# Building the block-diagonal operands of a state recurrence in four groups of chunks, with the sums on VectorE and the placement on ScalarE

## The chip, the cores and the metric

The kernel is one launch on one core of a Trainium2 chip. The metric is the device time of the launch in microseconds, the median of several runs. Beside the times there is one profiled execution with its trace: for every instruction the engine, its start and duration, and what released it. The engines are TensorE (PE, with its weight loads as PEld), VectorE (DVE), ScalarE (ACT), GpSimd (POOL) and SyncE (SP), which issues nearly all DMAs.

## The reference, cut to what matters

Two blocks of a network on 256 tokens of 1024 features, float32. The first block has a mixer with two branches, a gate and an output product, and a feed-forward layer. The second block has two layers, each with two gated feed-forward parts around a mixer with two attentions. The change lies in the first block's mixer, in its state-space branch:

```
u = rmsnorm(x); proj = u @ w_in; u_ssm, q, k, v = split(proj)       # 512 columns each
a = exp(lam * dt); b = ((a - 1) / lam) * (B_re + i B_im)            # 32 groups, 64 states, 16 channels
x_t = a * x_(t-1) + b u_t;  y_t = Re(C x_t) + D u_t                 # per group, over 256 tokens
y = gelu(y); y = y * sigmoid(y @ w_glu + b_glu)
```

The other branch is a stick-breaking attention over q, k, v (8 heads). The gates are `sigmoid(u @ w_gate + b_gate)`, eight weight blocks.

## The kernel before, in words

**Weights.** All products are float32 in three passes: each weight block of 1 MB is loaded by SP, ScalarE writes its high part (L538), VectorE its low part (L553), both in halves of 1024 columns, and TensorE multiplies high by high, high by low, low by high (L590 to L592). One feature-major block is 48 matmuls of 256 columns. In the first mixer up to three split blocks are held at a time.

**The order.** The tile framework is told to keep the order of emission, so each engine's queue is the order in which the program emits. In the first mixer the class `Flow` writes that order: each stream of work is a generator that yields an engine, a declared time and the buffers it needs (`acc`, `t2`, `t4`), or the name of a signal to wait for. `Flow` keeps a clock for each engine in these declared times, emits the piece that could start first (among pieces close together the one with the lowest priority number), and puts steps of the fillers, which are the large products, where TensorE would otherwise wait. One filler step is two tiles, six matmuls, counted as 2 x 0.327 us. The fillers come in this order: u0, u1 (the recurrence's inputs), qk0 to qk3, the values v, then a barrier "kz", then the eight gate blocks, a barrier "sg", and the rest. `f.free["POOL"] = 5.5` tells `Flow` that GpSimd is busy for 5.5 us with a fill that was emitted just before.

**The recurrence.** It runs over 64 steps of four tokens. `s5_load_bc` issues the DMAs of B and C in SP's queue, behind x, constants and the first three weight blocks. `s5_powers` makes the powers of a: `pw` and `dk`, [128, 4, 2, 16] each (power, real or imaginary, chunk). `s5_c` masks C into `cpad` on GpSimd (L1033, four products), transposes it on TensorE (L1041) and copies it back on ScalarE (L1043). Two operands are block-diagonal, [128, 2, 16, 4, 2, 16], 4096 columns: `s5bb` (B times dk) and `s5wT` (C times pw). Both are filled with zeros by GpSimd, s5bb at the start of the mixer (L1368), s5wT inside `s5_c` (L1049). `s5_part` then makes one of the four powers for all 16 chunks: two products of 512 columns on VectorE (L995), and four sums of 256 columns on 64 partitions on GpSimd, written straight into the diagonal blocks (L998, L999). There are four parts for B and four for C.

When all four parts of B are done, `s5_b` transposes s5bb (L1017, ScalarE copies at L1020) into `bT`, with a signal for each quarter, and `s5_k` multiplies s5bb by C's transpose (L1102, signal "kz"). `s5_states` (four groups of chunks) multiplies the inputs by bT (L1161), turns and scans them on VectorE and GpSimd, and adds their outputs with `s5wT` (L1205, L1208), once all four parts of C are there (signal "wT"). `s5_turns` makes the rotations `csT` (VectorE L1075 to L1078, ScalarE L1081 to L1083). `stick` is one head of the attention: two `t2` buffers from its first product until its last, which needs the values; heads run one at a time. The copies of the inputs u into the steps' layout are 16 ScalarE instructions of 32 partitions for each of u0 and u1 (L1141).

Of the kernel before, what the change touches and what calls it, by code (L numbers as in the profile page):

```python
# [25 lines left out]
# The tail of a layer: its last TAIL row blocks, row by row; the products after which the first row's two  # L26
# halves are transposed, in feed-forward layers and in the others.
# [3 lines left out]
# Of Flow: buffers, priorities, and what it weighs (times in us).  # L31
# [10 lines left out]
# The first block's later products: gates, glu and the two projections.  # L42
LATE = "g0 g1 g2 g3 g4 g5 g6 g7 lu a0 a1 s0 s1".split()
# The weight stream: blocks loaded in halves, tiles split ahead, split blocks at a mixer's end.
# [3 lines left out]
# When a feed-forward layer's first hidden columns are turned (without and with gate), and when the  # L48
# weights of a mixer's first products are taken.
# [4 lines left out]
def host_constants():  # L54
    """Tables that depend on the shapes alone."""
# [39 lines left out]
class Halves:  # L95
    """Columns of a row in two tiles."""
# [10 lines left out]
class Row:  # L107
    """The end of a layer for 128 tokens: their sums on top of the residual, the norm
    (of the root mean square, or of mean and variance when there is a bias) and the
    feature-major split of the result."""  # L110
# [31 lines left out]
    def finish(self):  # L142
        """Up to the scale of the rows; then self.piece(c0, c1) writes the result."""
# [26 lines left out]
    def turn(self, c0, c1, pool=None):  # L170
        """Transposes columns c0:c1 and splits the high parts; returns the low parts' step."""
        k, nc, b = self.k, self.k.nc, self.b
        n = (c1 - c0) // P
        t = slice(b * P, (b + 1) * P)
        ps = (pool or k.mm)("tp")
        for c in range(n):
            nc.tensor.transpose(ps[:, c * P:(c + 1) * P], self.out[:, b, c0 + c * P:c0 + (c + 1) * P], k.ident)  # L177
        q = slice(c0 // P, c1 // P)
        v = ps[:, :n * P].rearrange("p (c t) -> p c t", c=n)
        hi, lo = self.xs[0][:, q, t], self.xs[1][:, q, t]  # L180
        nc.scalar.activation(hi, v, AF.Copy)  # L181
        return lambda: nc.vector.tensor_tensor(lo, v, hi.bitcast(F32), OP.subtract)

    def early(self):
        """All of it but the transposes."""
# [8 lines left out]
    def late(self, head):  # L194
        """All of it, the next layer's work on the other tokens filling the wait."""
# [15 lines left out]
class FFHead:  # L211
    """The first 256 hidden columns of a feed-forward layer, token by token."""
# [40 lines left out]
class MixHead:  # L253
    """The first columns of a mixer's input product, token by token."""
# [21 lines left out]
def act(n, exp=False):  # L276
    """A ScalarE instruction's time, in us, for n columns."""
# [3 lines left out]
def dve(n, fast=False):  # L281
    """A VectorE instruction's time, in us, for n columns."""
# [3 lines left out]
class Flow:  # L286
    """An order of emission for streams of work that share the engines. A stream is a generator that
    yields (engine, time, resources...) before it emits that work, or the name of a signal to wait for;
    the next piece is the one that could start first by a model of the engines, and fillers (feature-major
    products) go where TensorE would wait. Each resource is a count of buffers with the times at which  # L290
    they come free."""
# [24 lines left out]
    def rest(self):  # L316
        """Puts off the current stream, whose products are too small to keep TensorE's clock up."""
# [6 lines left out]
    def start(self, s):  # L324
        """When a stream's next piece could start, or None."""
# [26 lines left out]
    def weight(self, e):  # L352
        """The next part of the weights' split, as a stream's piece."""
# [26 lines left out]
    def filler(self, t):  # L380
        """A step of the first filler."""
# [13 lines left out]
    def evac(self, engine, d, f):  # L395
        """Work that follows the filler's products."""
        self.evacs.append((self.free["PE"] + 0.65, engine, d, f))

    def open(self):
        """Whether a filler can go on."""  # L400
# [51 lines left out]
class Kern:  # L452
    def __init__(self, ctx, tc, A, out):
# [8 lines left out]
        self.blocks = []      # planned weight blocks, in the order of their use  # L462
        self.staged = []      # loaded, not yet split
        self.loaded = 0
        self.pieces = 0       # halves of blocks split so far
# [36 lines left out]
    def rowblk(self, w, r0, nk, c0, n):  # L502
        """nk chunks of 128 rows from r0, n columns from c0, as [128, nk, n]."""
# [26 lines left out]
    def high(self):  # L530
        """The high part of half a weight block."""
# [9 lines left out]
    def piece(self):  # L541
        """The low part of half a weight block, and the high part of the next."""
# [43 lines left out]
    def mm3(self, out, l, r, start, stop, **kw):  # L586
        """out (+)= l.T @ r, the operands split in high and low parts."""
# [6 lines left out]
    def split_from(self, hi, lo, src, scale=None):  # L594
        """hi, lo (float32r) from src (* scale)."""
# [8 lines left out]
    def fm_gen(self, key, xs, evac, alloc=None):  # L604
        """A feature-major block: [128, 256] sums per 128 columns, in PSUM tiles of
        two; evac(i, tile) follows each tile. Yields the tiles of work done."""
# [27 lines left out]
    def fill(self, tiles):  # L634
        """Emits about that much of the waiting work."""
# [9 lines left out]
    def tok_mm(self, o, w, xs, k0, b, c0, c1, first, last, **kw):  # L645
        """Adds a row block to the token-major sums o of the 128 tokens b, columns c0:c1."""
# [9 lines left out]
    def tok_first(self, o, ws, b, n):  # L656
        """The token-major sums o of n columns, the tokens' low parts last."""
# [15 lines left out]
    def tok_tail(self, accs, parts, rows, head, at):  # L673
        """The last row blocks (w, xs, k0): the first 128 tokens, then the others,
        each followed by the end of its row."""
# [24 lines left out]
    def bcast_row(self, src, n, name):  # L700
        """A row of DRAM on every partition."""
# [13 lines left out]
    def transpose_split(self, src, nchunk, xs):  # L715
        """src: [128 tok, 2, nchunk*128] -> split feature-major xs."""
# [155 lines left out]
    # The states' recurrence runs over 64 steps of four tokens each: state' = a^4 state + V [u], and  # L872
    # the outputs of a step are W state + K [u], with V, W and K made of B, C and the powers of a.
    # Its inputs and outputs sit on the partitions as (token of the step, channel of 32).
# [26 lines left out]
    def s5_powers(self, f):  # L901
        """The powers of a and what goes with them: s5c (parameters by state), pw, dk, tau4, r4."""
# [60 lines left out]
        cf = dk[:, 0]  # L963
# [9 lines left out]
        def cmul(out, x, y, n):  # L973
            """out = x * y, complex; x: n numbers per state chunk, y: one."""
# [9 lines left out]
        cmul(dk[:, 1:4], pw[:, 0:3], cf, 3)  # L984
# [3 lines left out]
    def s5_part(self, f, dst, x, y, k, s0, s1):  # L988
        """dst (block-diagonal) = y_k * x; s0, s1: the signs' operations."""
        nc = self.nc  # L990
        TT, GT = nc.vector.tensor_tensor, nc.gpsimd.tensor_tensor
        yield "DVE", 2 * dve(512), "t4"
        t = self.t4([P, 2, 2, 16, 16], "s5p")
        for i in range(2):
            TT(t[:, i], x, y[:, k, i, None, :, None].to_broadcast([P, 2, 16, 16]), OP.mult)  # L995
        yield "POOL", 2.8
# [1255 lines left out]
```

## Time and profile before

| | |
|---|---|
| median of 3 runs | 1560.99 us (1559.63 to 1564.06) |
| profiled execution, first to last instruction | 1560.2 us (no other time of it is listed) |
| mean granted TensorE clock | 0.994 |
| busy: TensorE, VectorE, ScalarE, GpSimd | 1534.7, 992.3, 773.2, 97.8 us |

The median stands 0.8 us above the span of the profiled execution. "Busy" of TensorE counts overlapping matmuls as one stretch, so a busy TensorE need not be at its peak; where the granted clock is low, the same matmuls take longer and count as busy all the while.

### The profile page before, as it was taken

To read this page: it belongs to the slowest core of one execution; us is meant where nothing else is said; L and a number is where in the kernel's file an instruction comes from. 1 tells how busy PE (TensorE), PEld (TensorE's weight loads), DVE (VectorE), ACT (ScalarE), POOL (GpSimd) and SP (SyncE) were. 2 spreads that over 40 slices of the span, in tenths; PEclk is the share of its full clock that TensorE was granted. 3 is DMA by queue.
4 is the path that set the end of the run, shared out by engine and by line. 5 is a ranking of instruction groups with operands and counts; after the bars stand their busy time and mean duration, and the time that the engine had idled before them with its cause. 6 is when DMAs were issued, how large, how long until landed. Compare 5 with 4: busy or idle time off the path is not lost.

```text
span 1560.2 us, 25562 instructions
## 1 busy us (share of the span) xinstructions
PE 1534.7 (98%) x10637; PEld 1418.5 (91%) x10637; DVE 992.3 (64%) x1572; ACT 773.2 (50%) x1259; POOL 97.8 (6%) x112
## 2 busy tenths in 40 slices
PE   8799999999999999999999999999999999999998
PEld 7699989989999998989999999999999999899997
DVE  7956776454654547778875445844557779864544
ACT  7455845444543435557654343534434567554342
POOL 2841000000000000000000000000000000000000
PEclk9899999999999999999999999999999999999999
DMA  7413355556564555532565655565546433565550
GB/s 215 154 62 122 136 197 186 197 172 207 179 225 163 186 183 176 192 103 88 188 216 189 204 175 189 191 210 170 185 152 216 136 108 125 181 225 189 188 190 28
DMA packets 188597, 265.24 MB, mean 170 GB/s; under 512 B 10441, under 2 KB 154817, under 8 KB 188482
## 3 DMA queue, kind: packets, MB, share of 16 engines
q1 hardware_dynamic: 186466, 256.27, 49.7%
q0 software_dynamic: 2016, 7.34, 1.4%
q8 instruction: 84, 1.38, 0.4%
q14 instruction: 31, 0.25, 0.0%
HBM read 262.55 MB, written 1.05 MB: 169 GB/s over the span
## 4 chain that ended last, share of the span: by engine, by line
PE 92%; DVE 4%; POOL 2%; ACT 1%; issue 1%; DMA 0%; DVEq 0%; SPq 0%; ACTq 0%
PE mm L590 16%; PE mm L591 16%; PE mm L592 16%; PE acc L591 8%; PE acc L592 8%; PE acc L590 8%; PE head L664 6%; DVE wsplit L553 1%; PE tp L177 1%; PE cps L1665 1%; PE in L590 1%; PE in L592 1%; PE in L591 1%; PE apt L1949 1%; PE mo L1887 1%
## 5 line engine op out<-in xcount | busy, mean ns | idle before, releaser
L553 DVE TENSOR_TENSOR wsplit<-st,wsplit 128x1024 fp32r<-128x1024 f32 (+1 forms) x482 | 562.0, 1210 | 184.4 <-ACT wsplit L538 184.0
L590 PE MATMUL mm<-xh,wsplit 128*128 128x256 f32 x2000 | 572.2, 286 | 0.0
L591 PE MATMUL mm<-xl,wsplit 128*128 128x256 f32 x2000 | 564.8, 282 | 0.0
L592 PE MATMUL mm<-xh,wsplit 128*128 128x256 f32 x2000 | 564.8, 282 | 0.0
L538 ACT ACTIVATE wsplit<-st 128x1024 fp32r<-128x1024 f32 (+1 forms) x482 | 471.7, 1036 | 30.6 <-DMA st<-in_ffn_wg_dram 11.9
L590 PEld LDWEIGHTS mm<-xh,wsplit 128*128 128x128 f32 x2000 | 378.9, 189 | 4.5 <-issue 1.1
L591 PEld LDWEIGHTS mm<-xl,wsplit 128*128 128x128 f32 x2000 | 379.0, 189 | 2.1
L592 PEld LDWEIGHTS mm<-xh,wsplit 128*128 128x128 f32 x2000 | 378.6, 189 | 0.2 <-DVE wsplit L553 0.2
L590 PE MATMUL acc<-wsplit,ffh 128*128 128x512 f32 x480 | 189.5, 395 | 0.0
L592 PE MATMUL acc<-wsplit,ffl 128*128 128x512 f32 x480 | 189.4, 395 | 0.0
L591 PE MATMUL acc<-wsplit,ffh 128*128 128x512 f32 x480 | 189.3, 394 | 0.0
L828 ACT ACTIVATE fff<-mm 128x512 f32<-128x512 f32 x55 | 32.9, 598 | 280.1 <-PE mm L592 280.1
L832 DVE TENSOR_TENSOR fff<-fff,mm 128x512 f32<-128x512 f32 x55 | 37.9, 688 | 174.4 <-PE mm L592 111.2
L598 ACT ACTIVATE ffh<-fff 128x512 fp32r<-128x512 f32 x55 | 34.8, 632 | 165.8 <-DVE fff L832 165.8
L592 PEld LDWEIGHTS acc<-wsplit,ffl 128*128 128x128 f32 x480 | 90.4, 188 | 21.0
L590 PEld LDWEIGHTS acc<-wsplit,ffh 128*128 128x128 f32 x480 | 90.4, 188 | 18.8
L591 PEld LDWEIGHTS acc<-wsplit,ffh 128*128 128x128 f32 x480 | 90.4, 188 | 18.7
L707 POOL TENSOR_TENSOR rowst<-rowst,neghalf 128x1 f32<-128x1 f32 x18 | 14.7, 817 | 1227.2 <-DVE rowst L154 946.8
L664 PE MATMUL head<-wsplit,xh 128*128 128x256 f32 (+2 forms) x416 | 66.1, 311 | 0.0
L664 PEld LDWEIGHTS head<-wsplit,xh 128*128 128x128 f32 x416 | 59.6, 188 | 3.5
L599 DVE TENSOR_TENSOR ffl<-fff,ffh 128x512 fp32r<-128x512 f32 x55 | 38.1, 693 | 38.4 <-ACT ffh L598 38.4
L181 ACT ACTIVATE xh<-tp 128x256 fp32r<-128x256 f32 (+1 forms) x46 | 18.6, 470 | 48.6 <-PE tp L177 48.6
(405 smaller groups left out, 1894.6 us busy)
## 6 DMA issues: line engine op xcount, KB each, us to landing
st<-in_ffn_wg_dram SPq DMA_DIRECT2D x44, 1024.0 KB, 5.6
st<-in_ffn_wu_dram SPq DMA_DIRECT2D x44, 1024.0 KB, 5.4
st<-in_ffn_wd_dram SPq DMA_DIRECT2D x44, 1024.0 KB, 5.0
st<-in_w_ff_dram SPq DMA_DIRECT2D x32, 1024.0 KB, 6.4
st<-in_w_in_dram SPq DMA_DIRECT2D x23, 1024.0 KB, 6.3
st<-in_w_out_dram SPq DMA_DIRECT2D x12, 1024.0 KB, 4.9
st<-in_w_gate_dram SPq DMA_DIRECT2D x8, 1024.0 KB, 5.5
st<-in_w_in_dram SPq DMA_DIRECT2D x10, 512.0 KB, 5.4
```

The source lines that it names most:

```text
L177: nc.tensor.transpose(ps[:, c * P:(c + 1) * P], self.out[:, b, c0 + c * P:c0 + (c + 1) * P], k.ident)
L181: nc.scalar.activation(hi, v, AF.Copy)
L538: self.nc.scalar.activation(self.split[i][0][:, a, b], self.staged[i][:, a, b], AF.Copy)
L553: self.nc.vector.tensor_tensor(lo[:, a, b], st[:, a, b], hi[:, a, b].bitcast(F32), OP.subtract)
L590: nc.tensor.matmul(out, lh, rh, start=start, stop=False, **kw)
L591: nc.tensor.matmul(out, lh, rl, start=False, stop=False, **kw)
L592: nc.tensor.matmul(out, ll, rh, start=False, stop=stop, **kw)
L598: nc.scalar.activation(hi, src, AF.Copy)
L599: nc.vector.tensor_tensor(lo, src, hi.bitcast(F32), OP.subtract)
L664: self.nc.tensor.matmul(o, l, r, start=i == 0, stop=i == len(ops) - 1)
L828: nc.scalar.activation(f, ps, AF.Silu if gated else AF.Relu)
L832: nc.vector.tensor_tensor(f, f, ps, OP.mult)
```

## The change

`s5_part` makes a group of four chunks for all four powers, instead of one power for all 16 chunks. VectorE does four products of 256 columns and both sums (256 columns each on 128 partitions) into a new `t2` buffer; ScalarE copies the sums into the diagonal blocks, in two instructions of 64 partitions and 512 columns. GpSimd does no sums. To allow this, `dk` is stored in reverse order of the powers, and its three products are made one by one. `s5_b` transposes each group as soon as it is placed and signals its quarter of `bT`; "bb" comes after the last transposes. "wT" is signalled by group, and `s5_states` waits for its own group alone. The zero fills of both operands move to the very start of the program, ahead of the first DMA issue: s5bb and a quarter of s5wT on GpSimd, three quarters of s5wT on VectorE. The line `f.free["POOL"] = 5.5` goes, and so does GpSimd's declared 3.4 us for s5wT's fill.

```diff
@@ s5_powers
-        cf = dk[:, 0]
+        cf = dk[:, 3]
...
-        cmul(dk[:, 1:4], pw[:, 0:3], cf, 3)
+        for k in range(3):
+            cmul(dk[:, 2 - k:3 - k], pw[:, k:k + 1], cf, 1)
@@ s5_part
-    def s5_part(self, f, dst, x, y, k, s0, s1):
+    def s5_part(self, f, dst, x, y, g, s0, s1):
-        TT, GT = nc.vector.tensor_tensor, nc.gpsimd.tensor_tensor
-        yield "DVE", 2 * dve(512), "t4"
-        t = self.t4([P, 2, 2, 16, 16], "s5p")
+        TT = nc.vector.tensor_tensor
+        js = slice(4 * g, 4 * g + 4)
+        yield "DVE", 4 * dve(256) + 2 * dve(256), "t4", "t2"
+        t = self.t4([P, 2, 2, 4, 4, 16], "s5p")
+        u = self.t2([P, 2, 4, 4, 16], "s5u")
         for i in range(2):
-            TT(t[:, i], x, y[:, k, i, None, :, None].to_broadcast([P, 2, 16, 16]), OP.mult)
-        yield "POOL", 2.8
+            for r in range(2):
+                TT(t[:, i, r], x[:, r, js, None, :].to_broadcast([P, 4, 4, 16]),
+                   y(i)[:, :, js].rearrange("p k j -> p j k")[..., None].to_broadcast([P, 4, 4, 16]), OP.mult)
+        TT(u[:, 0], t[:, 0, 0], t[:, 1, 1], s0)
+        TT(u[:, 1], t[:, 0, 1], t[:, 1, 0], s1)
+        f.put("t4")
+        yield "ACT", 2 * act(512)
         for a, h in enumerate((slice(0, 64), slice(64, P))):
-            GT(dst[h, 0, :, :, a], t[h, 0, 0], t[h, 1, 1], s0)
-            GT(dst[h, 1, :, :, a], t[h, 0, 1], t[h, 1, 0], s1)
-        f.cur["ready"] = max(f.cur["ready"], f.free["POOL"])
-        f.put("t4")
+            nc.scalar.activation(dst[h, :, js, :, a], u[h], AF.Copy)
+        f.put("t2")
@@ s5_b
-        for k in range(4):
-            yield from self.s5_part(f, self.bb[:, :, :, 3 - k].rearrange("p i j a c -> p i j c a"), self.s5bn,
-                                    self.dk, k, OP.subtract, OP.add)
+        for g in range(4):
+            yield from self.s5_part(f, self.bb, self.s5bn, lambda i: self.dk[:, :, i], g, OP.subtract, OP.add)
+            if g == 0:
+                self.bT = self.t16([P, 16, 2, P], "s5bT")
+            for j in (4 * g, 4 * g + 2):
+                yield "PE", 0.43, "acc"
...
+                yield "ACT", act(512)
+                nc.scalar.activation(self.bT[:, j:j + 2].rearrange("p j i s -> p (j i s)"), ps, AF.Copy)
+                f.put("acc")
+            f.sig("bT%d" % g)
         f.sig("bb")
...
@@ s5_c
-        yield "POOL", 3.4
-        self.wT = wT = self.t16([P, 2, 16, 4, 2, 16], "s5wT")
-        nc.gpsimd.memset(wT, 0.0)
...
-        for k in range(4):
-            yield from self.s5_part(f, wT[:, :, :, k].rearrange("p i j a c -> p i j c a"), cc, self.pw, k,
-                                    OP.add, OP.subtract)
+        for g in range(4):
+            yield from self.s5_part(f, self.wT, cc, lambda i: self.pw[:, :, i], g, OP.add, OP.subtract)
+            f.sig("wT%d" % g)
         f.put("t2")
-        f.sig("wT")
@@ s5_states
-        yield "wT"
+        yield "wT%d" % g
@@ first_block
         self.consts()
+        self.bb = self.t16([P, 2, 16, 4, 2, 16], "s5bb")
+        nc.gpsimd.memset(self.bb, 0.0)
+        self.wT = self.t16([P, 2, 16, 4, 2, 16], "s5wT")
+        nc.vector.memset(self.wT[:, 0], 0.0)
+        nc.vector.memset(self.wT[:, 1, :8], 0.0)
+        nc.gpsimd.memset(self.wT[:, 1, 8:], 0.0)
...
-        self.bb = self.t16([P, 2, 16, 4, 2, 16], "s5bb")
-        nc.gpsimd.memset(self.bb, 0.0)
-        f.free["POOL"] = 5.5
```

## Rows read from the trace of the kernel before

**Rows 1.** Windows of 10 us: busy by engine (instructions), granted clock, DMA share, GB/s.

```profile
core 0: us, PE busy (x) PEld busy (x) DVE busy (x) ACT busy (x) POOL busy (x), PEclk, DMA share, GB/s
...
30.00:40.00 10.00, 10.00 (x86) 10.00 (x86) 9.64 (x31) 9.77 (x24) 0.37 (x1) 1.00 0.43 132
...
50.00:60.00 10.00, 8.37 (x40) 7.75 (x40) 10.00 (x12) 6.26 (x9) 9.73 (x9) 0.66 0.42 124
60.00:70.00 10.00, 6.72 (x30) 5.27 (x30) 9.83 (x12) 0.78 (x2) 9.73 (x9) 1.00 0.27 91
70.00:80.00 10.00, 7.28 (x32) 6.26 (x33) 9.79 (x7) 3.08 (x4) 9.75 (x8) 0.66 0.67 206
```

**Rows 2.** Waits of TensorE, 40 to 100 us: total, times, longest.

```profile
PE s5ps L1017 <- POOL s5bb L998: 2.7, 1, 2.7
PE sc L1288 <- DVE sa L1284: 2.4, 1, 2.4
PE sz L1268 <- ACT H L1391: 2.4, 1, 2.4
PE s5ps L1017 <- POOL s5bb L999: 1.2, 1, 1.2
```

**Rows 3.** Groups of TensorE's instructions by line, 40 to 100 us.

```profile
L590 PE MATMUL mm<-xh,wsplit 128*128 128x256 f32 x45 | 14.1, 313 | 0.0
...
L590 PE MATMUL mm<-wsplit,xh 128*128 128x512 f32 x16 | 7.3, 454 | 0.0
```

**Rows 4.** The chain that ended last, in order of time: start, us, what.

```profile
94.46 0.81 PE s5k L1102 x8
```

**Rows 5.** Timeline of VectorE: start, us, instruction.

```profile
9.12 3.59 DVE L1352 COPY s5par<-s5par 16x128 f32<-16x128 f32 x1
...
24.74 4.00 DVE L950 TENSOR_SCALAR s5q<-s5q 128x16 f32<-128x16 f32 x1
...
38.20 1.28 DVE L995 TENSOR_TENSOR s5p<-s5bc,s5q 128x512 f32<-128x512 f32 x2
...
47.70 1.22 DVE L553 TENSOR_TENSOR wsplit<-st,wsplit 128x1024 fp32r<-128x1024 f32 x1
...
52.78 2.37 DVE L995 TENSOR_TENSOR s5p<-s5bc,s5q 128x512 f32<-128x512 f32 x2
...
66.46 0.42 DVE L1294 SCALAR_TENSOR_TENSOR szs<-const,szs 128x256 f32<-128x256 f32 x1
66.80 1.77 DVE L553 TENSOR_TENSOR wsplit<-st,wsplit 128x1024 fp32r<-128x1024 f32 x1
```

**Rows 6.** Timeline of GpSimd.

```profile
9.13 3.51 POOL L1368 MEMSET s5bb<- 128x4096 f32 x1
22.00 3.25 POOL L1033 TENSOR_TENSOR s5cpad<-s5bc,const 128x256 f32<-128x256 f32 x4 [9.36 <-DMA s5bc<-in_C_re_dram]
25.19 3.51 POOL L1049 MEMSET s5wT<- 128x4096 f32 x1
...
47.86 1.64 POOL L998 TENSOR_TENSOR s5bb<-s5p 64x256 f32<-64x256 f32 x1 [4.16 <-DVE s5p L995]
...
71.38 1.70 POOL L999 TENSOR_TENSOR s5bb<-s5p 64x256 f32<-64x256 f32 x1
...
81.82 0.74 POOL L999 TENSOR_TENSOR s5wT<-s5p 64x256 f32<-64x256 f32 x1
```

**Rows 7.** Timeline of TensorE.

```profile
15.34 0.58 PE L590 MATMUL mm<-xh,wsplit 128*128 128x256 f32 x1
...
19.13 0.41 PE L592 MATMUL mm<-xh,wsplit 128*128 128x256 f32 x1
...
25.50 0.60 PE L1041 MATMUL s5ps<-const,s5cpad 128*128 128x128 f32 x4
```

**Rows 8.** Timeline of ScalarE.

```profile
20.11 1.28 ACT L940 ACT_TABLE_LOAD   x1
...
23.56 4.48 ACT L1141 ACTIVATE u<-mm 32x128 f32<-32x128 f32 x16 [0.96 <-PE mm L592]
28.06 0.60 ACT L1043 ACTIVATE s5cT<-s5ps 128x512 f32<-128x512 f32 x1
```

More of the change, by code (lines that the diff above doesn't have):

```diff
@@ L1006, in s5_b @@
         yield "pw"
-        for k in range(4):
-            yield from self.s5_part(f, self.bb[:, :, :, 3 - k].rearrange("p i j a c -> p i j c a"), self.s5bn,
-                                    self.dk, k, OP.subtract, OP.add)
+        for g in range(4):
[4 more added lines that the diff above has]
+                yield "PE", 0.43, "acc"
+                ps = self.acc("s5ps")
+                for k in range(4):
+                    nc.tensor.transpose(ps[:, k * P:(k + 1) * P],
+                                        self.bb[:, k % 2, j + k // 2].rearrange("p i a c -> p (i a c)"), self.ident)
+                yield "ACT", act(512)
+                nc.scalar.activation(self.bT[:, j:j + 2].rearrange("p j i s -> p (j i s)"), ps, AF.Copy)
+                f.put("acc")
+            f.sig("bT%d" % g)
         f.sig("bb")
         f.put("t4")
-        self.bT = self.t16([P, 16, 2, P], "s5bT")
-        for j in range(0, 16, 2):
-            yield "PE", 0.43, "acc"
-            ps = self.acc("s5ps")
-            for k in range(4):
-                nc.tensor.transpose(ps[:, k * P:(k + 1) * P],
-                                    self.bb[:, k % 2, j + k // 2].rearrange("p i a c -> p (i a c)"), self.ident)
-            yield "ACT", act(512)
-            nc.scalar.activation(self.bT[:, j:j + 2].rearrange("p j i s -> p (j i s)"), ps, AF.Copy)
-            f.put("acc")
-            if j % 4 == 2:
-                f.sig("bT%d" % (j // 4))
     def s5_c(self, f):
@@ L1056, in s5_c @@
         yield "pw"
-        for k in range(4):
-            yield from self.s5_part(f, wT[:, :, :, k].rearrange("p i j a c -> p i j c a"), cc, self.pw, k,
-                                    OP.add, OP.subtract)
+        for g in range(4):
+            yield from self.s5_part(f, self.wT, cc, lambda i: self.pw[:, :, i], g, OP.add, OP.subtract)
+            f.sig("wT%d" % g)
         f.put("t2")
-        f.sig("wT")
     def s5_turns(self, f):
```

## The prediction

> **What bounds the kernel now.** I read the windows first. TensorE is busy nearly everywhere, so only a stretch where it isn't fed can give anything. That stretch lies between 48 and 80 us, inside the first block's mixer: TensorE's busy time falls to 6.72 us of 10 and its granted clock to 0.66 in two windows, while VectorE stands at 9.8 to 10.0 and GpSimd at 9.7 [rows 1]. Then the waits of TensorE: four between 40 and 100 us, 8.7 us in all, two for GpSimd's products in s5bb, one for a VectorE step of the first attention head, one for a ScalarE copy [rows 2]. The clock costs as well: 8.37 and 7.28 us busy at 0.66 in place of 1.00 is (8.37 + 7.28) x 0.34 = 5.3 us. That makes 14. The other way round: the stretch holds 135 products of 256 columns and 48 of 512 [rows 3], at a full-clock spacing of 0.12 and 0.23 us 27.3 us, and some 17 us of K, transposes, states and attention: 44 of 60, so 16 lost. I take 15, the most that can be had here, since after the end of K's products at 95.27 [rows 4] TensorE is dense and its work is the same in both kernels.
>
> Why VectorE and GpSimd are late: they slow each other. A pair of 512-column products takes VectorE 1.28 us with GpSimd idle and 2.37 beside GpSimd's sums; a weight's low part 1.22 and 1.77 [rows 5]. The sums, 32 of them, take mostly 1.0 to 1.7 us each and run almost without a break from 47.86 to 82.56 [rows 6], where the order written out by the kernel allows 2.8 us for four. The fills matter too: a VectorE instruction of 16 columns takes 4.00 us from 24.74, and a copy of 128 columns 3.59 from 9.12 [rows 5]; both end with a fill of GpSimd's, at 28.70 and 12.64 [rows 6].
>
> **Part by part.** *Fills.* s5bb whole and a quarter of s5wT go to GpSimd, three quarters of s5wT to VectorE, ahead of everything. GpSimd's 4096 columns took 3.51 us [rows 6], so its 5120 take 4.4; VectorE's 3072 are bounded by the same rate and by one column a nanosecond, 2.6 to 3.1. Both start below 1.4 us and end before 5, when both engines still wait for x. I cost them at nothing. If they excluded each other they would end near 8 and push the start back 2 us, which the wait for C below would swallow. Gained: VectorE isn't held at 9.12 and 24.74, some 3.4 and 3.8 us.
>
> *Sums and placement.* VectorE now does eight parts of six 256-column instructions. The nearest row has 0.42 us for 256 columns, of which some 0.08 overlaps the next: 48 x 0.34 = 16.3 us (bounds 48 x 0.30 and 48 x 0.43: 14.4 and 20.6). The 16 products of now cost 16 x 1.18 = 18.9 disturbed; 16 x 0.64 = 10.2 undisturbed [rows 5]. dk's products become twelve instructions of 0.2 in place of four, +0.7 with the shorter ones set off. The eight low parts in the stretch go from about 1.7 back to 1.2, -4. So VectorE is relieved by 6 us, and GpSimd of all 32 sums. ScalarE gets 16 placements of 512 columns on 64 partitions: nearest is 0.60 for 128x512, spacing 0.55, 8.8 us; the 32-partition copies at 0.28 give a lower bound of 4.5, 0.63 an upper of 10 [rows 8].
>
> The rows say that a 256-column instruction costs two thirds of a 512-column one. The Trainium skill ("VectorE: DVE Perf Modes", section Rules for kernel authors) says to minimize the number of instructions, not to worry about what is fused; that speaks against 48 in place of 16. If the number alone set the price, 48 x 0.64 = 31 us, VectorE would be done 14 us later than below and the sum would be near 1565; by the rows it is 16.3 and the sum the one below. I go by the rows and give this no chance of its own.
>
> *The order.* This decides. The removed line told the order that GpSimd is busy until 5.5. So cpad's products (declared 2.4) were entered at 5.5 to 7.9 and their transposes (L1041) at 8.1, behind 11 filler steps of six matmuls (0.654 each, from 0.75): 66 matmuls. The rows agree: 15.34 to 25.50 us holds some 24 at 0.21 and 42 at 0.12 [rows 7]. Now GpSimd is free at 0: cpad at 0.2 to 2.6, the transposes at 2.8, behind three steps, 18 matmuls. But cpad waits for the DMA of C_re until 22.00 and ends at 25.25 [rows 6], and nothing in the change moves that DMA: its place in SP's queue, behind six half blocks of weights and B, stays. TensorE starts its 18th matmul at 19.13 [rows 7] and then stands until cpad's third product, about 24.6: 5.1 us. What follows starts at the low clock again, as at 15.34: 18 matmuls more at 0.21 for 0.12, 1.7 us. Together 6.8.
>
> What is queued behind it: on TensorE u0's other 30 matmuls, done at about 31.1 in place of 23.4. On ScalarE the copy of the transposes (L1043) now stands ahead of the sine's table load, which goes from 20.11 [rows 8] to 26; the sines end near 28, and with VectorE's 3.6 us behind them and the 0.6 of dk the powers are there at 32.2 in place of 33.0. So the time won at GpSimd's fill is spent here. Then u0's copies take 4.48 us of ScalarE [rows 8], 31.1 to 35.7, and the high part behind them ends at 36.7; VectorE's next low part needs it and stands in front of csT, two more low parts and the first part of B. That part starts at 36.8 + 1.14 + 1.8 + 2.3 = 42.0, in place of 38.20 [rows 5].
>
> From there ScalarE is the tight engine: u1's copies, two high parts, csT's sines and a copy of keys come first, so the first placement is at 47.8 to 48.9. The order puts that group's transposes 22 steps of 0.71 us behind u0's end, at 46.8. TensorE waits 2.1 us more, and if the clock falls as it did after the 2.4 us at 51 [rows 1, 2], another 2.8 go: I take 4.5 (bounds 0 and 7). After that the engines run level: ScalarE's list up to B's fourth part (18 copies' worth of u 9, nine high parts 9, four evacuations 2.2, sines 4, seven placed parts 7.7, six copies of bT 3) is 35 us, to 66; VectorE's ends near 67; TensorE gets to the fourth group's transposes at about the same time. bb is whole near 67 in place of 73.08 [rows 6], and K's products follow while the values' fillers last.
>
> *Sum.* -15 + 6.8 + 4.5 = -3.7 us against a span of 1560.2: 1556.5. The median of the three runs, 1560.99, is 0.8 above that span; I leave the 0.8 to the range.
>
> **Rivals.** *A, the wait for C costs little: clearly faster.* The lost time comes out of a stretch in which TensorE waits today, and the first placement is in time. For it: it waits at 68 to 73 us for just these operands [rows 2], and a later TensorE waits less. Against: without those waits its own work is the bound. 1560.2 - 15 + 5.1 = 1550, to 1547 with a bit of the clock.
>
> *B, ScalarE takes what the others give back: no change.* For it: 9.77 us busy of 10 between 30 and 40 [rows 1], u copies of 4.48 where the order allows 2.55, and now 8.8 more. If it falls behind by another 4 us over the later groups: 1556.5 + 4 = 1560.5.
>
> *C, the parts run out of t2 buffers: slower.* A part now holds one from its products to its placement. Four are free by then; two groups of states, which may start as soon as bT0 and bT1 are there, hold one each until K, and an attention head takes two and keeps them until the values are evacuated. If the head is entered before B's fourth part, that part waits for the values, near 85 us. Its chain (2.0 + 1.1 + 2 of transposes and copies) and eight pieces of K at 0.81 follow with nothing to fill in, as the gates' fillers wait for K: 11.6 us. That replaces the 4.5, with a fall of the clock of 2.8 on top: 1560.2 - 15 + 6.8 + 11.6 + 2.8 = 1566.4. It decides from the point where the head's piece comes before that part in the order. Against it: by the declared times B's fourth part comes at 36, and two buffers aren't free together before 42.
>
> **Chances.** Forecast 0.52 (its own range 1553 to 1560), A 0.20, B 0.15, C 0.13. The range 1548 to 1564 leaves out the low end of A and nearly all of C. About 0.3%, 4.7 us, is what can be told from no change; counted from the span 1560.2 and the median alike, the line is near 1556. Faster is A and half of the forecast, 0.46; same the other half and nearly all of B, 0.39; slower C and a rest of B, 0.15.
>
> **What would show it.** A wait of TensorE of about 5 us from 19 us on, at cpad's transposes, released by GpSimd; no VectorE instruction of 4 us before 30; the first 256-column product near 42; placements of 0.5 to 0.6 us; low parts at 1.22; nothing on GpSimd from 30 to 45; K's products ending near 85 to 90. Wrong would be: no wait at 19 us (then toward A), 256-column instructions over 0.43, placements near 1 us, or TensorE idle behind the values' last product (C).

## The result, and the profile after

The changed kernel takes 1573.78 us (median of 4 runs, 1571.49 to 1574.76) against 1561.42 for the kernel before beside it (4 runs): ratio 1.0074, 95% interval 1.006 to 1.0088. The forecast was 1556.5 with a range up to 1564. It is slower, and by more than the whole range allowed.

| | before | after |
|---|---|---|
| span of the profiled execution, us | 1560.2 | 1571.4 |
| mean granted clock | | 0.987 |
| last product of the last head (`so`) starts, us | 166.00 | 177.88 |
| first product of `out` starts, us | 205.24 | 217.28 |

From TensorE's timeline of the kernel before, and of the changed one:

```profile
166.00 0.38 PE L1310 MATMUL so<-szs,vt 128*64 128x128 f32 x2
205.24 0.39 PE L590 MATMUL acc<-wsplit,xh 128*128 128x512 f32 x1
```

```profile
177.88 0.38 PE L1312 MATMUL so<-szs,vt 128*64 128x128 f32 x2
217.28 0.40 PE L590 MATMUL acc<-wsplit,xh 128*128 128x512 f32 x1
```

The loss is complete when the first block's output product starts: 217.28 - 205.24 = 12.0 us, against 11.2 in the span. So only the stretch up to there has to be read. Windows of the changed kernel, TensorE alone (busy, instructions, granted clock, DMA share, GB/s):

```profile
core 0: us, PE busy (x), PEclk, DMA share, GB/s
20.00:30.00 10.00, 4.81 (x29) 0.66 0.90 243
...
50.00:60.00 10.00, 10.00 (x78) 0.88 0.53 184
60.00:70.00 10.00, 8.90 (x58) 0.83 0.40 117
70.00:80.00 10.00, 10.00 (x65) 1.00 0.28 94
...
90.00:100.00 10.00, 10.00 (x67) 0.84 0.33 104
...
120.00:130.00 10.00, 9.21 (x60) 0.87 0.35 110
130.00:140.00 10.00, 10.00 (x46) 0.50 0.25 89
140.00:150.00 10.00, 10.00 (x50) 0.60 0.22 64
```

The hole of 50 to 80 us [rows 1] is filled: 28.9 us busy of 30 where 22.4 were. But 130 to 150 us is new, and this is the trap in the view. TensorE reads as busy 10.00 of 10, and 96 instructions stand where 151 did before:

```profile
130.00:140.00 10.00, 10.00 (x79) 1.00 0.32 107
140.00:150.00 10.00, 10.00 (x72) 1.00 0.48 159
```

In the changed kernel the clock is 0.50, the lower of its two levels, 1.2 GHz, and 0.60, a mean of both. Nothing waits in these 20 us. The waits of TensorE from 20 to 240 us, the two longest:

```profile
engine line waited for: us in total, times, longest us
PE s5ps L1047 <- POOL s5cpad L1039: 6.8, 1, 6.8
PE s5ps L1022 <- ACT s5bb L1007: 3.6, 3, 1.9
```

The four waits of before [rows 2] are gone; the wait of 6.8 was forecast at 5.1, the first of the other three (1.92) at 2.1. From here on I add up, over windows of 10 us, what TensorE lost: idle time, and busy time x (1 - clock). From 10 to 230 us that is 12.3 + 5.3 = 17.7 before and 13.2 + 16.6 = 29.9 after (added before rounding). The idle time hardly moved; the clock took 11.3. Nor did the loss arise in the stretch that the forecast added up: from 10 to 90 us it is 16.5 before and 16.1 after, behind 90 us it is 1.2 before and 13.8 after, 11.9 of that by the clock.

Most of the early work went as forecast. VectorE, GpSimd, TensorE and ScalarE of the changed kernel:

```profile
9.00 0.21 DVE L1360 COPY s5par<-s5par 16x128 f32<-16x128 f32 x1
...
24.05 0.54 DVE L950 TENSOR_SCALAR s5q<-s5q 128x16 f32<-128x16 f32 x1
...
42.16 1.43 DVE L1000 TENSOR_TENSOR s5p<-s5bc,s5q 128x256 f32<-128x256 f32 x4
43.62 0.42 DVE L1002 TENSOR_TENSOR s5u<-s5p 128x256 f32<-128x256 f32 x1
...
77.52 1.29 DVE L1154 TENSOR_TENSOR s5m<-s5b,csT 128x512 f32<-128x512 f32 x2 [3.96 <-PE s5b L1163]
78.72 2.52 DVE L1000 TENSOR_TENSOR s5p<-s5bc,s5q 128x256 f32<-128x256 f32 x4
```

```profile
0.74 3.51 POOL L1330 MEMSET s5bb<- 128x4096 f32 x1 [0.29 <-POOLq L2246]
4.19 0.95 POOL L1334 MEMSET s5wT<- 128x1024 f32 x1
...
23.34 2.37 POOL L1039 TENSOR_TENSOR s5cpad<-s5bc,const 128x256 f32<-128x256 f32 x4 [14.28 <-DMA s5bc<-in_C_re_dram]
```

```profile
25.19 1.11 PE L1047 MATMUL s5ps<-const,s5cpad 128*128 128x128 f32 x4 [6.80 <-POOL s5cpad L1039]
28.59 0.60 PE L1047 MATMUL s5ps<-const,s5cpad 128*128 128x128 f32 x4
48.37 0.66 PE L1022 MATMUL s5ps<-const,s5bb 128*128 128x128 f32 x4 [1.92 <-ACT s5bb L1007]
```

```profile
31.37 4.47 ACT L1143 ACTIVATE u<-mm 32x128 f32<-32x128 f32 x16 [1.55 <-PE mm L592]
...
47.06 1.25 ACT L1007 ACTIVATE s5bb<-s5u 64x512 f32<-64x512 f32 x2
...
60.69 2.01 ACT L538 ACTIVATE wsplit<-st 128x1024 fp32r<-128x1024 f32 x2 [3.27 <-PE mm L592]
62.60 1.25 ACT L1007 ACTIVATE s5bb<-s5u 64x512 f32<-64x512 f32 x2
...
73.63 1.26 ACT L1007 ACTIVATE s5bb<-s5u 64x512 f32<-64x512 f32 x2
...
82.14 1.27 ACT L1007 ACTIVATE s5bb<-s5u 64x512 f32<-64x512 f32 x2
```

The fills end at 5.1 and hold nobody (3.59 and 4.00 us before [rows 5] are 0.21 and 0.54). The first products come at 42.16 (forecast 42.0) and the first placement at 47.06 (47.8 to 48.9). The next three come at 62.6, 73.6 and 82.1, not at 67. So K's products, in the chain that ended last, read:

```profile
87.33 2.60 PE s5k L1104 x24
90.72 1.90 PE s5k L1104 x16
93.47 2.79 PE s5k L1104 x24
```

These 64 still come at 0.11 us each, the full clock; it falls behind them (0.84 from 90 to 100 us). Before, they stood eight at a time between other products, the last eight at 94.46 [rows 4]. And the states' outputs, with their turns, form one block at 128 to 147 us, with 18 large products among them (one line of TensorE's timeline; 16 products at 0.23 us each):

```profile
128.84 3.62 PE L1163 MATMUL s5b<-u,s5bT 128*128 128x64 f32 x16
```

### The profile page after: what moved, and what is told of

It is laid out like the page before. It is cut to its first block, busy times and chain, and to the rows that moved or that the text cites. A ratio compares the mean times of both kernels' runs of the same rounds, so it can differ in the third digit from the quotient of the medians.

```text
span 1571.4 us, 25598 instructions
## 1 busy us (share of the span) xinstructions
PE 1544.6 (98%) x10637; PEld 1434.9 (91%) x10637; DVE 989.9 (63%) x1614; ACT 782.7 (50%) x1275; POOL 62.5 (4%) x80
## 3 DMA queue, kind: packets, MB, share of 16 engines
q1 hardware_dynamic: 186466, 256.27, 49.7%
## 4 chain that ended last, share of the span: by engine, by line
PE 92%; ACT 3%; DVE 2%; issue 0%; POOL 0%; DVEq 0%; ACTq 0%; POOLq 0%
PE mm L590 16%; PE mm L591 16%; PE mm L592 16%; PE acc L591 8%; PE acc L590 8%; PE acc L592 8%; PE head L664 6%; PE cps L1670 1%; ACT wsplit L538 1%; PE tp L177 1%; PE in L590 1%; PE in L592 1%; PE in L591 1%; PE apt L1954 1%; PE s5b L1163 1%; PE ys L1210 1%
## 5 line engine op out<-in xcount | busy, mean ns | idle before, releaser
L590 PEld LDWEIGHTS mm<-xh,wsplit 128*128 128x128 f32 x2000 | 387.2, 194 | 5.3 <-issue 1.3
L591 PEld LDWEIGHTS mm<-xl,wsplit 128*128 128x128 f32 x2000 | 387.2, 194 | 2.3 <-DVE xl L182 0.4
L592 PEld LDWEIGHTS mm<-xh,wsplit 128*128 128x128 f32 x2000 | 387.0, 194 | 0.0
L181 ACT ACTIVATE xh<-tp 128x256 fp32r<-128x256 f32 (+1 forms) x46 | 18.6, 469 | 45.8 <-PE tp L177 45.6
```

The lines of the kernel that those rows point to most:

```text
L590: nc.tensor.matmul(out, lh, rh, start=start, stop=False, **kw)
L591: nc.tensor.matmul(out, lh, rl, start=False, stop=False, **kw)
L592: nc.tensor.matmul(out, ll, rh, start=False, stop=stop, **kw)
```

## The experiments

Theories. **1:** lateness behind the early wait for C. **2:** the states start early, their buffers run short, and their outputs heap up at the low clock. **3:** ScalarE is overfull. **4:** the values' fillers end before K's products, which then stand among small products alone, and the clock falls. **5** (formed after the first eight runs): the gates' products are a fixed stock; what an order uses of them ahead of the last head is missing behind it.

| run | ratio to before (95%) | last `so`, us | products behind it | first of `out`, us | lost 10 to 160 / 160 to 230 |
|---|---|---|---|---|---|
| kernel before | 1 | 166.0 | 318 | 205.2 | 16.8 / 0.9 |
| changed kernel | 1.0074 (1.0060 to 1.0088) | 177.9 | 318 | 217.3 | 29.1 / 0.8 |
| e1_pool_busy | 1.0058 (1.0041 to 1.0075) | 163.7 | 408 | 213.1 | 26.3 / 0 |
| e2_states_after_k | 1.0101 (1.0086 to 1.0116) | 174.2 | 378 | 219.9 | 28.7 / 0.4 |
| e5_both | 1.0061 (1.0039 to 1.0083) | 166.9 | 390 | 214.1 | 29.7 / 0.6 |
| e3_before_pool_free | 1.0002 (0.9992 to 1.0011) | 166.6 | 318 | 205.8 | 18.0 / 0.9 |
| b1_before_k_late | 1.0082 (1.0060 to 1.0104) | 173.3 | 348 | 215.1 | 28.3 / 0 |
| k1_k_groups | 1.0105 (1.0087 to 1.0124) | 170.3 | 270 | 219.3 | 15.3 / 14.7 |
| k2_k_groups_pool | 1.0056 (1.0035 to 1.0077) | 163.4 | 270 | 213.1 | 10.3 / 16.3 |
| k3_k_groups_both | 1.0083 (1.0062 to 1.0104) | 165.0 | 270 | 213.7 | 9.5 / 14.6 |
| k4_heads_first | 0.9993 (0.9982 to 1.0005) | 162.0 | 348 | 204.2 | 15.0 / 1.2 |
| k5_no_rest | 1.0060 (1.0043 to 1.0078) | 170.0 | 312 | 214.2 | 19.2 / 5.6 |
| k6_heads_first_both | 1.0033 (1.0022 to 1.0045) | 167.2 | 348 | 209.4 | 21.3 / 0 |
| a4_gates_open | 1.0110 (1.0090 to 1.0130) | 169.7 | 270 | 218.7 | 11.7 / 14.7 |
| a5_split | 1.0089 (1.0072 to 1.0106) | 167.1 | 270 | 215.7 | 12.7 / 14.8 |
| a6_split_pool_heads | 1.0046 (1.0032 to 1.0061) | 164.6 | 306 | 208.8 | 13.9 / 6.9 |
| f1_early_fills | 0.9976 (0.9965 to 0.9988) | 162.9 | 318 | 202.3 | 13.8 / 1.6 |
| f2_early_fills_free | 0.9999 (0.9990 to 1.0009) | 167.0 | 318 | 206.5 | 16.0 / 0.8 |
| p1_parts_alone | 1.0071 (1.0054 to 1.0087) | 162.7 | 408 | 211.7 | 25.0 / 0 |

The fourth column counts the products between the last head and `out` in TensorE's order; the others are from the traces. Behind the first of `out` the profiled executions differ too: it takes 1353 to 1355 us to the end in the five kernels with 318 products, 1356 to 1360 in the others. The table does not explain that part.

**e1, e2, e5: the two early suspects.** e1 puts the line `f.free["POOL"] = 5.5` back into the changed kernel; e2 lets a group of states start behind K; e5 does both.

```diff
         f = Flow(self, dict(acc=5, t2=4, t4=5, grp=2, sunit=SUNIT))
+        f.free["POOL"] = 5.5
```
```diff
     def s5_states(self, f, g, u4, ys):
         yield "u%d" % (g // 2)
+        yield "kz"
```

> The changed kernel with the line that tells the order that GpSimd is busy until 5.5 put back, and nothing else. Theory 1 (the early entry of cpad's transposes makes TensorE wait 6.8 us for C, and its delay makes ScalarE's high parts wait for split blocks to be released, with the placements queued behind them): the wait at 25 us is gone, ScalarE's high parts no longer wait for TensorE, and the time falls from 1573.8 to 1558 to 1562. Theory 2 (groups of states start as soon as their quarter of bT is there, hold t2 buffers, cannot get two more, and their outputs come late in one heap of small products at the low clock): only the wait goes, 7 to 8 us, 1565 to 1567, and a stretch of low clock after 115 us stays. Theory 3 (ScalarE simply has too much to do in this stretch): 1566 or more and ScalarE over 9 us busy in each window from 40 to 80.

> The changed kernel with the groups of states held until K's products are done (one wait for the signal kz more in the order), the early wait for C left as it is. Theory 1: little moves, 1571 to 1574. Theory 2: the first scan comes soon after K instead of at 119 us, the outputs are spread among the gates' products, the granted clock stays at 1.00 from 110 to 150 us (0.87, 0.50 and 0.60 before this edit in its three windows from 120), and the time falls by 8 to 10, to 1564 to 1566. Theory 3: no change.

> Both edits together in the changed kernel. Theories 1 and 2 each as a full account give what their own edit gives alone (1558 to 1562, or 1564 to 1566). If both are parts of it, the gains add: 1573.8 - 8 - 9 = 1556 to 1558. Theory 3: over 1564.

e1's wait for C is 0.5 us and its first part comes 7 us earlier, at 35.20; the time falls by 2.7 us only. e2 costs some 3 us more, though the clock stands at 1.00 from 120 to 160 us, as theory 2 had it: the low clock has moved to 90 to 120 us (0.50, 0.50, 0.55), where K's products are. Theories 1 and 2 fall as causes of the whole. What all three share is in e1's windows:

```profile
80.00:90.00 10.00, 8.97 (x36) 0.50 0.34 107
90.00:100.00 10.00, 10.00 (x41) 0.50 0.00 0
100.00:110.00 10.00, 10.00 (x40) 0.50 0.33 105
```

**e3: the wait for C in the kernel before.** That kernel without the line:

> The kernel before with only the line gone that tells the order that GpSimd is busy until 5.5. TensorE waits for cpad at about 19 to 25 us, 5 to 7 us. Theory 1: the delay goes through to the end, 1565 to 1570 against 1561.4. If the wait is taken out of the 8.7 us for which TensorE waits later anyway: 1560 to 1563.

TensorE waits 5.8 us for C and the first part is 4.5 us late (42.73 for 38.20), yet the time stays. The wait is taken out of the ones at 50 to 80 us.

**b1: one signal in the kernel before.** `f.sig("bb")`, on which K's products wait, moves behind the last transposes, where the changed kernel has it. Nothing else is touched.

```diff
-        f.sig("bb")
         f.put("t4")
...
             if j % 4 == 2:
                 f.sig("bT%d" % (j // 4))
+        f.sig("bb")
```

> The kernel before, with its signal bb moved behind the last transposes, as in the changed kernel; its parts, fills and placement stay. The order then has all K's products in one row with three pieces of the attention, behind the last product of the values. Theory 4: K's products take 0.21 us instead of 0.10, some 20 to 25 us at the low clock, and the time rises from 1562 to 1570 to 1575, which is the whole of the change's loss. If the products' place in the order doesn't matter: 1562 to 1564.

1.0082: by itself this costs as much as the whole change (9.9 us up to `out`, the rest behind it). Its TensorE, with no fillers between these rows:

```profile
91.67 7.03 PE L1102 MATMUL s5k<-s5cT,s5bb 128*128 128x32 f32 x32
98.52 1.20 PE L1288 MATMUL sc<-sa,const 128*128 128x256 f32 x2
```

32 products of K in 7.03 us are 0.22 each; the chain of before has eight in 0.81, about 0.10 [rows 4]. Theory 4's mechanism is real in this order. In the changed kernel K's products kept 0.11, and the low clock came behind them.

**k1, k2, k3: K's products spread out again.** In the changed kernel, K's four products of a group may start when that group is placed (k2 adds the line of e1, k3 that and the edit of e2).

```diff
@@ s5_b @@
+            f.sig("bb%d" % g)
@@ s5_k @@
-        yield "bb"
...
+            if j % 4 == 0:
+                yield "bb%d" % (j // 4)
```

> The changed kernel with K's products entered by group of chunks, as soon as that group of s5bb is placed, and nothing else. Theory 4 (the fillers end before K's products begin, because the signal bb now comes after the last transposes and the gates wait for K; K's, the attention's and the states' small products then run alone, TensorE never empties but its clock falls to 1.2 GHz): K's pieces lie among large products, the clock stays at 1.00 from 85 to 105 us and after 120, and the time falls from 1573.8 to 1558 to 1563, the early wait for C remaining. Theory 1 (lateness behind the wait for C): at most 3 us, 1570 or more. Theory 2 (states early and t2 short): 1570 or more.

> As the run before this one, with the line that tells the order that GpSimd is busy until 5.5 put back as well. Theory 4: the two low stretches go as there, and the wait for C with them: 1549 to 1555, faster than the kernel before (1562). Theories 1 and 2: as the edit of that line alone, 1571.

> As the run before this one, with the groups of states also held until K is done. Theory 4: 1548 to 1556, since the heap of K's products is gone either way. Theory 2: better than the run without it by 5 or more. Theory 1: 1570.

If theory 4 were all, these would lie at 1548 to 1563; they lie at 1571.7 to 1578.1. The low clock did go (k2 lost 6.2 us from 40 to 160 us where the changed kernel lost 19.7), and the time did not. The waits of k2 behind 160 us say where it went:

```profile
PE mm L590 <- ACT sg L1252: 3.5, 1, 3.5
PE mm L590 <- ACT oah L1539: 3.0, 1, 3.0
PE mm L591 <- DVE oal L1541: 2.1, 1, 2.1
```

Behind the last head comes a chain on ScalarE and VectorE (gelu, then `sg`, the glu, the joined heads). Before, 78 gate products stood in front of `sg`'s first (166.31 to 175.66); k2 has 30. Spread-out heads and K's products had used up the others. This gave theory 5.

**k4, k5, k6, a4: the stock of products.** k4 is k2 with the heads ahead of the recurrence's groups in the order, k6 the same on k3, k5 is k2 with another pause. a4 is the changed kernel with its gate products no longer held until K.

```diff
@@ k4, k6 @@
-PSTICK = 3
+PSTICK = 2
@@ k5 @@
-REST = 0.3
+REST = 0.0
@@ a4 @@
-        late.append("kz")
```

> The version with K's products entered by groups and GpSimd's model busy until 5.5 us, with one number changed: the heads of the attention come ahead of the recurrence's groups in the order (PSTICK 2 for 3). Theory 5, from the traces of that version: the clock's loss between 40 and 160 us is gone there (2.7 us by the windows, 15.0 in the changed kernel), but the gates' products, which the spread-out heads and K's products have used up, are missing behind the last head: 30 of them are left behind its last product and TensorE waits 3.5 us for the gelu's result, 3.0 and 2.1 for the joined heads', at low clock in between, 16.3 us in all. With the heads first, 348 products instead of 270 stand behind the last head in the order: 78 at 0.12 us are 9.4 us, so the waits of 3.5, 3.0 and 2.1 go and most of the low clock with them. 1553 to 1559 us. Rival, theory 1 (lateness behind C and the parts themselves): the order behind 160 us doesn't matter, 1568 to 1572. Rival 6: the heads, now early, wait for the values or for ScalarE between 60 and 100 us and the low clock comes back there: 1562 to 1570.

> The same version (K's products by groups, GpSimd's model busy until 5.5 us) with PSTICK left at 3 and the pause behind each small product of the recurrence taken out of the model (REST 0 for 0.3): 312 products are left behind the last head instead of 270 (42 at 0.12 us are 5.0 us). Theory 5: part of the tail's 16.3 us comes back, 1559 to 1565. Theory 1: 1568 to 1572. If the small products then stand closer together and the clock falls on them: 1566 to 1574.

> The version with K's products by groups, GpSimd's model busy until 5.5 us and the groups of states behind K's products, with the heads first (PSTICK 2): 348 products behind the last head instead of 270. Theory 5: the tail's 14.6 us go, 7.7 us between 40 and 160 us stay: 1554 to 1561. Theory 1: 1570 to 1575.

> The changed kernel with one line less: the gates' products no longer wait in the order for K's last product, so that they stand between K's products and behind them (in the order five groups of 6 between K's products, which had none). Theory 4: the low clock at 90 to 100 us goes and that at 130 to 150 us becomes shorter. Theory 5: what is used there is missing behind the last head (270 left instead of 318, 48 at 0.12 us are 5.8 us), so TensorE waits behind 165 us for the gelu's result by 3 to 4 us and for the joined heads' by 5, and the time stays at 1570 to 1578. If theory 5 is wrong and only the small products' company counts: 1560 to 1566.

k4 takes 10 us off k2 with one number, to 1561.77: the same as before. The range of theory 5 (1553 to 1559) was too good, because rival 6 took a part: one wait for the values' copy (2.6 us) and a low clock between 80 and 100 us (7.2 us lost to the clock from 40 to 160). k6 missed its range too, at 1567.6, with 12.4 us of clock. k5 missed theory 5's range and lies in the one named for the clock: 10.5 us of clock are lost from 40 to 160 us, 0.50 at 90 to 100. a4 is the cleanest. Its clock is 1.00 in every window from 20 to 170 us (two of them below), and by its median, 1578.76, it is the slowest of all, with k2's waits of 3.5, 3.0 and 2.1 at the end.

```profile
130.00:140.00 10.00, 9.57 (x74) 1.00 0.60 208
140.00:150.00 10.00, 10.00 (x78) 1.00 0.43 149
```

**a5, a6: why the operand was late.** s5_b's transposes become a stream of their own, so that a group's products don't stand behind the transposes of the group before. a6 adds the line of e1 and the heads first.

```diff
@@ s5_b @@
             yield from self.s5_part(f, self.bb, self.s5bn, lambda i: self.dk[:, :, i], g, OP.subtract, OP.add)
+            f.sig("bb%d" % g)
+        f.put("t4")
+
+    def s5_bt(self, f):
+
+        nc = self.nc
+        for g in range(4):
+            yield "bb%d" % g
             if g == 0:
                 self.bT = self.t16([P, 16, 2, P], "s5bT")
...
         f.sig("bb")
-        f.put("t4")
```

> The changed kernel with the states' operand built in a stream of its own, so that a group's products and placement no longer stand behind the transposes of the group before. If the order is what made it late, the fourth placement, at 82.1 us in the changed kernel, comes at 64 to 72; if ScalarE's queue is, at 78 to 83. In this order K's products stand between groups of 6 of the gates' products, so by theory 4 the low clock goes; but only 270 products are left behind the last head, so by theory 5 the time is gone at the end: 1570 to 1578. If the operand's lateness was the whole loss: 1560 to 1565.

> The same with GpSimd's model busy until 5.5 us (C's transposes stand behind 48 more products and find C there) and the heads ahead of the recurrence (PSTICK 2): 306 products behind the last head. Fourth placement at 57 to 65 us by the order, 70 or later by ScalarE's queue. Theory 5: no wait for C (6.8), no low clock at K's products, a tail 12 products short of before (1.4 us): 1556 to 1562. Rival: the end is as with 270 left, 1568 to 1574.

a5's fourth placement:

```profile
63.81 1.26 ACT L1007 ACTIVATE s5bb<-s5u 64x512 f32<-64x512 f32 x2
```

18 us earlier, and before the 67 forecast: the order made it late, not ScalarE's speed; theory 3 falls. And a5 has hardly a loss left up to 160 us (3.8 us from 40 on), no low clock at K, and is as slow as the changed kernel. a6 missed its range by 6 us: 306 products are still too few (waits of 1.6, 1.1 and 2.0 at the end), and 8.1 us of clock remain. The lower end of its rival's range is met by the time, not by the end of the stretch, which lost 6.9 us and not 14.7.

**f1, f2, p1: the two parts of the change apart.** f1 and f2 are the kernel before with the fills alone at the start (f2 without the line f.free). p1 is the changed kernel with the fills where they were and with that line.

```diff
@@ first_block @@
         self.consts()
+        self.bb = self.t16([P, 2, 16, 4, 2, 16], "s5bb")
+        nc.gpsimd.memset(self.bb, 0.0)
+        self.wT = self.t16([P, 2, 16, 4, 2, 16], "s5wT")
...
@@ s5_c @@
-        yield "POOL", 3.4
-        self.wT = wT = self.t16([P, 2, 16, 4, 2, 16], "s5wT")
-        nc.gpsimd.memset(wT, 0.0)
```

> The kernel before with one part of the change alone: both operands are zeroed at the start, on GpSimd and VectorE as in the changed kernel; the parts stay as they were (by token, summed and placed by GpSimd), and TensorE's order is that of before, instruction for instruction. Prediction's own step: the fills are worth the wait at the powers that they hold VectorE for, which nothing behind it makes up for or loses: 1558 to 1562. Theory 5: as many products stand behind the last head as before, so nothing is lost there, same or faster by up to 3 us. Rival: GpSimd, freed of 3.4 us of zero fill in the middle, places the parts earlier and the waits of before (2.7 and 1.2 for the operand) go: 1554 to 1559.

> The same, and GpSimd's model free from the start as in the changed kernel: C's transposes then stand 52 products of the gates' kind earlier in TensorE's order, and all else in it is as before. By what the kernel before did without that line (ratio 1.0002) the wait for C of 5 to 7 us is taken out of later waits: 1559 to 1563, like the run beside it. Theory 1 (lateness behind C is what costs): 1564 to 1568.

> The change without its other part: the parts by groups on VectorE and ScalarE, but both zero fills where and when the kernel before had them, on GpSimd, with its model busy until 5.5 us. If the two parts add up, the parts alone cost what the changed kernel with GpSimd's model busy costs (ratio 1.0058) plus what the early fills give (0.9976): about 1.008, 1572 to 1577. In the order, all of K's products stand among small products of the heads, with 408 products left behind the last head: by theory 4 the granted clock is 0.5 there for some 20 us. If the early fills only help the kernel before: 1568 to 1572.

f1, at 1557.59 us against 1561.63, beats both kernels. VectorE of f1:

```profile
24.38 0.54 DVE L950 TENSOR_SCALAR s5q<-s5q 128x16 f32<-128x16 f32 x1
...
34.37 1.28 DVE L995 TENSOR_TENSOR s5p<-s5bc,s5q 128x512 f32<-128x512 f32 x2
```

The 4.00 of [rows 5] is 0.54, the first products come 3.8 us earlier (38.20 before), and all behind them: the last `so` by 3.1, `out` by 2.9. The time is in the range of f1's rival, but that rival's mechanism is not shown: the two waits for the operand are 1.3 and 1.2 us where 2.7 and 1.2 were, and the first head's wait is 4.8 where 2.4 was. f2 gives it back: the table load of its sines starts at 27.22 instead of 20.50, behind the wait for C of 7.0 us. p1 has 1.0071 where the sum of the parts gave 1.008; the two parts add up within the interval.

## Why the prediction was wrong

**The term of -15 failed.** "I take 15, the most that can be had here, since after the end of K's products at 95.27 [rows 4] TensorE is dense and its work is the same in both kernels." The losses of 50 to 80 us did go: 13.0 us of idle time and clock before, 3.8 after. Up to 90 us the account is -0.4 us where -3.7 was forecast. What failed is the premise: behind 90 us, where the prediction saw no difference, TensorE loses 13.8 us in place of 1.2, 11.9 of it because it runs at the low clock. The work there is the same in amount, not in order.

What a gain ahead of the heads is worth depends on that order, as the table shows. From the last `so` to `out` it takes 39.2 to 39.4 us in all five kernels with 318 products behind the last head (the changed kernel too), 41.9 to 42.2 with 348, 45.8 with 378, 47.2 with 390, 49.0 and 49.4 with 408: some 0.11 us for each product more. With fewer it gets longer again, 44.2 with 306 and 312, 48.7 to 49.7 with 270: there, waits and a low clock take the place of the missing ones. The kernel before stood near the optimum: 78 gate products cover its chain behind the last head, with a wait of 0.7. Early fills under the same order keep their gain (f1). An order that spreads the heads and K's products out uses up that stock sooner (k1 to k3, a4, a5); with the heads earlier as well it does not, and k4 is back at the time of before. The stock is why the repairs do not pay, and not the changed kernel's own loss: that one has its 318, and reaches the last head 11.9 us late.

**The order behind K failed with it.** The prediction let "K's products follow while the values' fillers last". In the changed kernel K starts with the last of them. There is a tail as in rival C, without waiting for buffers and nearly without idle time, but it lies later: 1.7 us of clock are lost at 90 to 110 us, just behind K, and 10.2 at 120 to 150, where the states' outputs now stand together. That the clock falls on small products with few fillers between them is what b1 (one signal moved) and a4 (fillers between them, and 1.00 throughout) show. What drove the outputs together is not separated: k1 (K's products by groups), a4 (no hold on the gates) and e2 (no early states) each leave 120 to 150 us at 1.00.

**"bb is whole near 67" failed**, by 16 us (82.14 + 1.27), and for the order, not the engine (a5). I had costed each engine's list and not the one stream in which a group's products follow the transposes of the group before. But a5 is no faster with this step mended, so the time does not hang on it alone.

**Right:** the fills at nothing; the place of the wait for C (6.80 us where 5.1 were forecast, as C came at 23.34 and not 22.00, and 1.6 of clock where 1.7 were); the powers' gain "spent here", which f1 against f2 shows; a part's six instructions at 0.34 to 0.36 us by their spacing; the first placement, 1.92 us of wait and 2.7 of clock from 50 to 70 us, 4.6 where 4.5 were taken. What I did not see is that the fills were worth 4 us by themselves, f1's result, and that the removed line then costs it again.

**The rivals.** A's condition, that the wait for C costs nothing, holds in the kernel before (e3, 1.0002) and not with the fills early (f2 against f1, 0.9999 against 0.9976). B's term did not come about: a5 places all of B by 65 us with the same list on ScalarE. C had the right sign for 13 in 100 and the right kind of stretch, small products with little to fill in, but the wrong place, K, and another price, mostly waits for buffers and not the clock.

The rows show the granted clock at 0.50 in the same window in which TensorE is busy for 10.00 of 10 us. The Trainium skill ("TensorE: Matmul & The Clock Gate", section Part 1: The HAM clock gate) ties the halved clock to how busy the array has been and warns of idle gaps; here the longest wait from 100 to 150 us is 0.6 us, so a wait is not the only thing to look for.

## What to carry to other kernels

Where an order mixes a latency chain with a fixed stock of filler work, the end is set by when the chain ends and how much filler is left behind it. Count both before pricing a wait that is removed, and read the stretch behind it in the new order before taking it as unchanged. Read the granted clock beside the busy share: a stretch that is busy throughout can be losing half. And where a change has two parts, time each alone: here one gave 0.24%, and the other took 0.7%.

## What the runs showed of the hardware

A zero fill on GpSimd holds a VectorE instruction of 16 columns for 3.98 to 4.00 us (L950 in the kernel before, e3 and p1); the same instruction takes 0.54 where the fill has been moved (changed kernel, f1, f2). Stretches in which most of TensorE's products had 32 to 128 columns, with few of 256 among them, ran at the granted clock 0.50 for whole windows (e1: 80 to 110 us; the changed kernel: 130 to 140) while its busy time read 9 to 10 of 10. Gate products of 256 columns among them came 0.21 us apart instead of 0.12. K's 64 products of 32 columns in the changed kernel, with only the heads' products between them, still ran at 0.11 us each (87.33 to 96.26 us); in b1, and at the clock 0.50, at 0.22.
